# One program order on all engines, from the trunk to the first up tiles, with second steps put off by a product

## The chip, the cores and the metric

The kernel runs on one core of one Trainium2 chip. The metric is device time in microseconds (us) of one execution; a number given for a kernel is the median of several executions. TensorE is called PE, VectorE DVE, ScalarE ACT, GpSimd POOL and SyncE SP, as in the profile.

## The reference

One layer of a streaming encoder is applied to 1024 prompt tokens and to 32 sample tokens, with the same weights, and a last norm follows. All is fp32, the model width is 1024.

```
def trunk_layer(x, attn_core, conv_left, mem_k, mem_v, ...):
    h = rms_norm(x, g_mix)
    q, k, v, ch, cb, cc, ga, gb = jnp.split(h @ w_in, SPLITS, axis=-1)
    a = attn_core(q, k, v) @ w_attn_out              # sliding window, 16 heads of 64
    ...                                              # conv: depthwise, width 3, over cc * ch
    bo = (cb * conv) @ w_conv_out
    x = x + (sigmoid(ga) * a + sigmoid(gb) * bo) @ w_mix_out
    hc = rms_norm(x, g_cross)
    cq = hc @ w_cq                                   # 4 heads of 64
    p = softmax(cq . mem_k * 0.125)                  # 256 memory tokens
    x = x + (p . mem_v) @ w_co
    hm = rms_norm(x, g_mlp)
    x = x + square(relu(hm @ w_up)) @ w_down         # hidden width 4096
```

## The kernel before

Activations lie transposed: 128 features on the partitions, tokens along the free axis. The 1056 tokens are cut into three chunks of 384, 384 and 288 columns; the sample's 32 tokens are the last of chunk 2. Every fp32 operand is split in two fp32r parts, a high part (a copy on ACT) and a low part (source minus high part, on DVE): `split`, lines 115 and 116. A product is one output tile of 128 features for one chunk: eight blocks of the inner dimension with three matmuls each, high weight by high activation, high by low, low by high (`gemm`, lines 167 to 169), 24 matmuls in all. Each weight panel (`wr`) is loaded by SP, split into `wh` and `wl` two products ahead of its use, and for every second panel the low part is kept in DRAM and loaded again for the later chunks (line 141 copies its high part).

The program is a list of items, each a function with the weights it wants; `run` goes through them. A tile scheduler then orders the instructions of each engine, by its own estimates of time. From the trunk to the first up tiles only PE is held to the program's order:

```
in_order = tc.manual_schedule(engines={mybir.EngineType.PE})
```

The **trunk** has eight `conv_out` and eight `mix` products for each chunk. A conv_out product is multiplied by a gate (DVE, line 747), an addend loaded from DRAM is added (POOL, line 748), and the sum is split into M (ACT and DVE, lines 115 and 116). The eight M tiles are the activations of mix. A mix product is added to x (DVE, line 762), scaled by a gain and split into Y (lines 241 and 242), and squared into a running sum (`square_acc`, lines 234 to 238).

Chunk 0's sixteen products come first. After that the products are **fillers**, numbered from 0: chunk 1's sixteen, chunk 2's sixteen, and then the first eight up products of each chunk. `cross_steps(c, base, ...)` hangs the cross-attention of chunk c between them, with base 0, 16 and 32: `at(i, step)` puts a step behind filler i.

- Row statistics: `chunk_col` (at base) sums the squares with a matmul against ones and makes the reciprocal root as a column; `chunk_row` (at base + 1) multiplies an identity by that column, block by block (ACT line 208 for the high part, DVE line 209 for the low part), and two matmuls per block against ones (lines 210 and 211, tile pr) turn it into a row R. The same pair comes again at base + 16 and base + 17 for the MLP's norm, so that the second pair of a chunk and the first of the next stand behind the same fillers.
- `do_cq`: two products for the queries.
- A head, class `Cross`: `scores` (six matmuls of 256 columns, tile sc; line 837), the maximum on DVE (nmx, line 840), three exponentials on ACT (line 842), normalization on DVE; two fillers later `turn` (PE transposes into pt, ACT copies the high part PTh, DVE subtracts the low part PTl); another filler later `values` (tile o, line 873), which is copied, added and split on ACT and DVE (lines 875 to 888). Heads start at the fillers `starts` from base: 3, 5, 7, 9, and 3, 4, 6, 7, 9 in chunk 2, where the sample's head is the first.
- `do_co` (at base + 13 and + 14): two halves of four output tiles each, six matmuls a tile (lines 902 to 904), each followed by an addition to x on DVE (line 906). Two tiles of a half share one PSUM buffer.

`mem_load` (behind filler 0), `mem_load_s` (behind filler 16) and the sample head itself load keys and values through a single buffer `mkr` and split them on ACT and DVE (mkh, mkl, mv). `normed_split` makes the MLP's input of a tile (line 931), stores it, and splits it (lines 933 and 935); eight for chunk 0 lie behind fillers 18 to 25 and eight for chunk 1 behind 34 to 39. `combine_n` and `combine` build sums of such tiles for the paired up products that follow.

## Time and profile before

| | |
|---|---|
| median of 3 runs | 1869.71 us |
| lowest and highest | 1868.11 and 1870.54 us |
| the profiled execution | 1866.0 us |
| its span | 1864.2 us |
| its mean granted PE clock | 0.988 |
| trunk to first up tiles in it | from about 816 to 1232 us |

The profile comes from one execution of its own. Its time is 1.8 us more than the span that the trace covers. A row of a timeline gives the start and the length in us, the engine and the source line, the output and input tiles, their shapes, and in brackets the idle time before it with what ended it. In a row of waits stand the engine, its tile and line, what it waited for, and then the total in us, the number of waits and the longest. A line can be that of a helper: line 116 is every low part that `split` makes, so the tiles' names tell them apart.

### The profile page before, as it was taken

The numbers are of one execution on the slowest core, as the hardware profiler recorded it, in microseconds if no ns is written. First come the engines' busy times: TensorE is split into PE (matmuls) and PEld (weight loads), VectorE is DVE, ScalarE is ACT, GpSimd is POOL, SyncE is SP. The second block draws the span as 40 slices with busy tenths as digits, with TensorE's granted clock in tenths as the row PEclk, the third lists the DMA queues.
The fourth block names the chain that finished last, engine by engine and source line by source line (L and its number), as shares of the span: only waits on it lengthen the run. The fifth ranks groups of instructions, "written<-read, shape, count | busy, mean of one in ns | idle before, by whom it ended". The sixth has DMA issues, their size and how long they took to land. (4 is left out here: it accounts for less than half of the span.)

```text
span 1864.2 us, 29594 instructions
## 1 busy us (share of the span) xinstructions
PE 1808.6 (97%) x11364; PEld 1787.9 (96%) x11364; DVE 1054.8 (57%) x2011; ACT 718.9 (39%) x1414; POOL 351.6 (19%) x381
## 2 busy tenths in 40 slices
PE   7999999999999999999999989899999999999997
PEld 7999999999999999999998889899999999999997
DVE  7766767757654224236575857656555674242255
ACT  8543435334343103223455645532222353030134
POOL 3211010201100000014232221473444000000032
PEclk9999999999999999999999999999999999999998
DMA  4411111212223125146655756643333574131243
GB/s 185 138 64 58 61 55 61 72 51 70 69 81 114 62 92 169 46 142 237 199 184 187 230 183 225 232 162 109 115 97 106 190 248 144 52 116 46 69 146 129
DMA packets 113934, 232.77 MB, mean 125 GB/s; under 512 B 13536, under 2 KB 76672, under 8 KB 113664
## 3 DMA queue, kind: packets, MB, share of 16 engines
q1 hardware_dynamic: 111488, 227.72, 36.5%
q10 hardware_dynamic: 2304, 3.15, 0.5%
q8 instruction: 90, 1.47, 0.3%
q14 instruction: 52, 0.43, 0.1%
HBM read 184.34 MB, written 46.48 MB: 124 GB/s over the span
## 5 line engine op out<-in xcount | busy, mean ns | idle before, releaser
L115 ACT CAST wh<-wr 128x1024 fp32r<-128x1024 f32 x200 | 210.0, 1050 | 503.0 <-PE acc L168 366.7
L167 PE MATMUL acc<-X,wh 128*128 128x384 f32 (+1 forms) x1200 | 390.4, 325 | 6.9 <-ACT wh L115 6.9
L168 PE MATMUL acc<-X,wh 128*128 128x384 f32 (+1 forms) x1200 | 387.8, 323 | 2.2 <-DVE X L242 2.2
L169 PE MATMUL acc<-X,wl 128*128 128x384 f32 (+1 forms) x1200 | 386.8, 322 | 0.3 <-DVE wl L116 0.3
L167 PE MATMUL acc<-Y,wh 128*128 128x384 f32 (+1 forms) x1008 | 328.2, 326 | 0.4 <-ACT Y L933 0.4
L168 PE MATMUL acc<-Y,wh 128*128 128x384 f32 (+1 forms) x1008 | 327.6, 325 | 0.2 <-DVE Y L935 0.2
L169 PE MATMUL acc<-Y,wl 128*128 128x384 f32 (+1 forms) x1008 | 327.1, 325 | 0.0
L116 DVE TENSOR_TENSOR wl<-wr,wh 128x1024 fp32r<-128x1024 f32 x200 | 270.7, 1354 | 65.3 <-ACT wh L115 63.8
L167 PEld LDWEIGHTS acc<-X,wh 128*128 128x128 f32 x1200 | 226.3, 189 | 7.5 <-ACT wh L115 6.9
L168 PEld LDWEIGHTS acc<-X,wh 128*128 128x128 f32 x1200 | 226.5, 189 | 3.9 <-DVE X L242 3.4
L169 PEld LDWEIGHTS acc<-X,wl 128*128 128x128 f32 x1200 | 226.2, 189 | 0.8 <-DVE wl L116 0.8
L167 PEld LDWEIGHTS acc<-Y,wh 128*128 128x128 f32 x1008 | 191.0, 189 | 0.7 <-ACT Y L933 0.7
L168 PEld LDWEIGHTS acc<-Y,wh 128*128 128x128 f32 x1008 | 190.9, 189 | 0.4 <-DVE Y L935 0.4
L169 PEld LDWEIGHTS acc<-Y,wl 128*128 128x128 f32 x1008 | 190.8, 189 | 0.0
L238 POOL TENSOR_TENSOR xacc<-xacc,ct 128x384 f32<-128x384 f32 (+1 forms) x62 | 80.0, 1291 | 366.7 <-ACT ct L236 364.1
L167 PE MATMUL acc<-M,wh 128*128 128x384 f32 (+1 forms) x320 | 106.2, 332 | 2.8 <-ACT M L115 2.8
L168 PE MATMUL acc<-M,wh 128*128 128x384 f32 (+1 forms) x320 | 106.0, 331 | 1.5 <-DVE M L116 1.3
L169 PE MATMUL acc<-M,wl 128*128 128x384 f32 (+1 forms) x320 | 105.5, 330 | 0.0
L748 POOL TENSOR_TENSOR ct<-ct,ld 128x384 f32<-128x384 f32 (+1 forms) x21 | 24.8, 1181 | 382.6 <-DVE ct L747 350.3
L1167 DVE TENSOR_TENSOR Gb<-acc,Gb 128x384 f32<-128x384 f32 (+1 forms) x60 | 31.4, 523 | 112.5 <-PE acc L169 112.5
L115 ACT CAST PTh<-pt 128x512 fp32r<-128x512 f32 (+3 forms) x94 | 46.0, 516 | 123.1 <-PE pt L536 122.2
L167 PE MATMUL acc<-H,wh 128*128 128x288 f32 (+1 forms) x256 | 80.7, 315 | 0.0
(292 smaller groups left out, 3485.7 us busy)
## 6 DMA issues: line engine op xcount, KB each, us to landing
wr<-in_w_down SPq DMA_DIRECT2D x56, 512.0 KB, 3.2
wr<-in_w_in SPq DMA_DIRECT2D x50, 512.0 KB, 3.3
wr<-in_w_up SPq DMA_DIRECT2D x48, 512.0 KB, 3.6
wl<-wl_d SPq DMA_DIRECT2D x28, 512.0 KB, 4.0
wr<-in_w_conv_out SPq DMA_DIRECT2D x24, 512.0 KB, 3.9
wr<-in_w_mix SPq DMA_DIRECT2D x24, 512.0 KB, 4.5
ct<-hid_d SPq DMA_DIRECT2D x64, 192.0 KB, 3.7
hid_d<-lt SPq DMA_DIRECT2D x48, 192.0 KB, 1.9
```

The costliest lines, as they stand in the source:

```text
L115: act.copy(hi, src)
L116: dve.tensor_sub(lo, src, hi.bitcast(F32))
L167: pe.matmul(out, wh[:, a], hi, start=(k == 0), stop=False)
L168: pe.matmul(out, wh[:, a], lo, start=False, stop=False)
L169: pe.matmul(out, wl[:, a], hi, start=False, stop=(k == len(acts) - 1))
L238: pool_e.tensor_tensor(acc, acc, sq, op=ALU.add)
L748: (dve if f == NF - 1 else pool_e).tensor_tensor(t, t, t1, op=ALU.add)
L1167: dve.tensor_add(x, a, x)
```

## The change

Line numbers below are those of the kernel before, unless the diff shows code that is new.

- From the trunk to the first up tiles, PE, DVE, ACT, POOL and SP are all held to the program's order.
- `later(fn)` puts a step on a list; `run` empties it after the next product's weights have been issued and before that product's own steps. Put off in this way are: the split of M (but for the last of eight), the low part of Y and of normed tiles, the low part of the queries, both low parts PTl, the normalization of the scores, the rest of `values` behind its first copy, the splits of the memory keys and values, and the sums of `combine_n` and `combine`.
- Memory keys and values are loaded one by one through two buffers: the prompt's keys behind the fourth, sixth, eighth and tenth product of chunk 0 and its values behind the twelfth and fourteenth, the sample's keys behind the other heads of chunk 2.
- Addends of conv_out and mix are loaded two ahead; one weight panel is fetched ahead of its turn.
- Heads start one filler earlier, the queries' evictions come after both cq products, co comes one filler earlier, and the sample's head is the last of chunk 2.
- The row is made by `row_parts`: the column is split into two parts on DVE, two 384-wide multiplications of a broadcast identity follow, and two matmuls. Its second use per chunk is at base + 16, so that it no longer shares fillers with the next chunk's first.
- ACT's function tables for Exp and Sqrt are loaded by a dummy operation ahead of their use.
- The store of a normed tile goes from ACT's queue to SP's; the low part of N1 goes from POOL to DVE.

```diff
     def run():
         for fn, keys in plan:
-            fn(*[next_w(k) for k in keys])
+            ws = [next_w(k) for k in keys]
+            if keys:
+                put_off_done()
+            fn(*ws)
...
+    def row_parts(c):
+        n, blocks = CH[c][1], BLOCKS[c]
+        pr = ps.tile([P, n], F32, tag="pt", bufs=2, name=nm("pr"))
+        rh, rl = (misc.tile([P, 3], F32R, tag=x, bufs=2, name=nm(x)) for x in ("st_h", "st_l"))
+        dve.tensor_copy(rh, RC[c])
+        dve.tensor_sub(rl, RC[c], rh.bitcast(F32))
+        dh, dl = tmp(n, F32R), tmp(n, F32R)
...
+        for d, r in ((dh, rh), (dl, rl)):
...
+            dve.tensor_tensor(d[:, : full * P].rearrange("p (b t) -> p b t", b=full), eyes, rs, op=ALU.mult)
...
+        pe.matmul(pr, ones_r, dh, start=True, stop=False)
+        pe.matmul(pr, ones_r, dl, start=False, stop=True)
+        return pr
...
+    def split_later(hi, lo, src):
+        act.copy(hi, src)
+        later(lambda: dve.tensor_sub(lo, src, hi.bitcast(F32)))
...
             t = tmp(n)
             dve.tensor_mul(t, a, sg[c][f])
-            (dve if f == NF - 1 else pool_e).tensor_tensor(t, t, t1, op=ALU.add)
             mg[c][f] = (mslot(n), mslot(n))
-            split(*mg[c][f], t)
+            if f == NF - 1:
+                dve.tensor_add(t, t, t1)
+                split(*mg[c][f], t)
+            else:
+                pool_e.tensor_tensor(t, t, t1, op=ALU.add)
+                later(lambda: split(*mg[c][f], t))
...
             for b in range(G):
                 act.activation(stl[:, b], sc[:, b], AF.Exp, bias=nmx[:, b : b + 1], accum_out=den[:, b : b + 1])
-            dve.reciprocal(rec, den)
-            for b in range(G):
-                dve.tensor_scalar_mul(stl[:, b], stl[:, b], rec[:, b : b + 1])
+            def norm():
+                dve.reciprocal(rec, den)
+                for b in range(G):
+                    dve.tensor_scalar_mul(stl[:, b], stl[:, b], rec[:, b : b + 1])
+            later(norm)
...
-                split(ph, pl, pt[:, :, P - w :])
+                split_later(ph, pl, pt[:, :, P - w :])
...
     def normed_split(c, f):
         t = tmp(CH[c][1])
-        pin(dve.scalar_tensor_tensor(t, x1[c][f], col(G_MLP + f), R[c], op0=ALU.mult, op1=ALU.mult))
-        hi, lo = xm[c][f] = (yslot(c), yslot(c))
-        act.copy(hi, t)
-        act.dma_start(xn_d[c][:, f], t)
-        pin(dve.tensor_sub(lo, t, hi.bitcast(F32)))
+        dve.scalar_tensor_tensor(t, x1[c][f], col(G_MLP + f), R[c], op0=ALU.mult, op1=ALU.mult)
+        sp.dma_start(xn_d[c][:, f], t)
+        xm[c][f] = (yslot(c), yslot(c))
+        split_later(*xm[c][f], t)
...
-        two_parts("N1", k, b11, pool_e)
...
+            two_parts("N1", k, b11, dve)
...
-        units = [Cross(c, h) for h in ([0, 1, 2, 3] if c < 2 else [4, 0, 1, 2, 3])]
+        units = [Cross(c, h) for h in ([0, 1, 2, 3] if c < 2 else [0, 1, 2, 3, 4])]
         at(base, lambda: chunk_col(c))
-        at(base + 1, lambda: chunk_row(c))
+        at(base + 1, lambda: chunk_scale(c), lambda: later(lambda: table(AF.Exp)))
         for j in range(2):
-            at(base + 2, (do_cq(c, j), ("w_cq", j)))
+            at(base + 1, (do_cq(c, j), ("w_cq", j)))
...
-        at(base + stats_at, lambda: chunk_col(c))
-        at(base + stats_at + 1, lambda: chunk_row(c))
+        at(base + 14, lambda: later(lambda: table(AF.Sqrt)))
+        at(base + 15, lambda: chunk_col(c))
+        at(base + 16, lambda: chunk_scale(c), all_waiting)
...
-    in_order = tc.manual_schedule(engines={mybir.EngineType.PE})
...
+    in_order = tc.manual_schedule(engines={ET.PE, ET.DVE, ET.Activation, ET.Pool, ET.SP})
...
+        if f in (3, 5, 7, 9):
+            item(lambda h=(f - 3) // 2: load_key(pkeys, mk_d[h // 2, 64 * (h % 2) : 64 * (h % 2) + 64]))
+        if f in (11, 13):
+            item(lambda j=(f - 11) // 2: load_val(pvals, mv_d[j], f"pv{j}"))
-    cross_steps(0, 0, [3, 5, 7, 9], 13, 16)
+    cross_steps(0, 0, [2, 4, 6, 8], 12)
...
-    cross_steps(1, 16, [3, 5, 7, 9], 13, 16)
-    cross_steps(2, 32, [3, 4, 6, 7, 9], 13, 16)
+    cross_steps(1, 16, [2, 4, 6, 8], 12)
+    starts = [2, 3, 5, 6, 8]
+    cross_steps(2, 32, starts, 12)
+    for h in range(4):
+        at(32 + starts[h], lambda h=h: load_key(skeys, io["cmem_k"][h]))
...
     for i, f in enumerate((0, 4, 1, 5, 2, 6, 3, 7)):
-        at(18 + i, lambda f=f: normed_split(0, f))
-        at((34, 35, 35, 36, 37, 37, 38, 39)[i], lambda f=f: normed_split(1, f))
+        at(17 + i, lambda f=f: normed_split(0, f))
+        at(32 + i, lambda f=f: normed_split(1, f))
```

## The prediction

> **What bounds the kernel now.** I began with the page of the profile: how long, and which engine.

> ```profile
> span 1864.2 us, 29594 instructions
> PE 1808.6 (97%) x11364; PEld 1787.9 (96%) x11364; DVE 1054.8 (57%) x2011; ACT 718.9 (39%) x1414; POOL 351.6 (19%) x381
> ```

> TensorE (PE) is busy for 1808.6 of 1864.2 us, so the kernel can only gain what PE idles or runs at a lowered clock. Next I cut the span into stages: ahead of the trunk, the four stretches of the trunk (conv_out and mix of chunk 0 and then the cross-attention of chunks 0, 1 and 2 with the first up tiles), and what follows. The last four rows are short stretches that I use below.

> ```profile
> 0.00:816.00 816.00, 803.12 (x5170) 793.86 (x5171) 465.09 (x1080) 330.14 (x749) 82.62 (x154) 1.00 0.25 86
> 816.00:942.00 126.00, 120.04 (x676) 118.09 (x675) 76.42 (x111) 55.48 (x92) 38.40 (x28) 0.97 0.63 211
> 942.00:1036.00 94.00, 87.27 (x543) 84.86 (x542) 61.88 (x116) 52.88 (x103) 30.44 (x28) 0.98 0.60 195
> 1036.00:1130.00 94.00, 82.27 (x504) 78.83 (x503) 64.55 (x117) 50.75 (x101) 26.23 (x27) 0.93 0.56 188
> 1130.00:1232.00 102.00, 95.44 (x610) 92.84 (x609) 72.29 (x129) 51.19 (x102) 46.17 (x40) 0.97 0.74 251
> 1232.00:1864.00 632.00, 620.46 (x3871) 619.44 (x3869) 314.58 (x461) 178.47 (x269) 127.80 (x106) 0.99 0.36 118
> 929.54:939.98 10.44, 10.44 (x65) 10.41 (x64) 7.76 (x14) 6.26 (x14) 2.03 (x2) 1.00 0.64 213
> 1027.42:1036.42 9.00, 8.81 (x66) 8.36 (x65) 8.88 (x18) 6.73 (x17) 2.37 (x3) 1.00 0.88 281
> 855.40:862.20 6.80, 5.30 (x16) 4.42 (x16) 3.51 (x7) 2.19 (x4) 0.00 (x0) 0.63 0.87 308
> 1114.00:1124.00 10.00, 5.41 (x18) 4.84 (x19) 4.50 (x7) 4.52 (x11) 1.00 (x1) 0.66 0.52 172
> ```

> In each row stand the length, then the busy time of PE, of its weight loads, of DVE, ACT and POOL, and the granted clock. In the trunk PE idles for 6.0 + 6.7 + 11.7 + 6.6 = 31.0 us. One minus the clock, times the length, gives 3.8 + 1.9 + 6.6 + 3.1 = 15.4 us lost to the clock. That is all that a change of the trunk can win, about 46 us. DVE is at 61 to 71% there and ACT at 44 to 56%: neither is full, so in this stage latencies decide, and the order in which a queue meets them. The waits of PE in the trunk say which:

> ```profile
> PE pr L210 <- ACT ct L208: 7.1, 5, 1.9
> PE sc L837 <- ACT mkh L115: 3.5, 1, 3.5
> PE co L902 <- DVE Gb L906: 3.3, 3, 2.1
> PE o L873 <- DVE PTl L116: 3.1, 3, 1.5
> PE acc L167 <- ACT M L115: 2.8, 3, 1.3
> PE co L902 <- DVE Ga L906: 2.8, 3, 1.6
> PE co L902 <- ACT Y L882: 2.1, 1, 2.1
> PE co L903 <- DVE Y L888: 1.8, 3, 0.8
> PE acc L168 <- DVE M L116: 1.3, 2, 1.0
> PE pr L211 <- DVE ct L209: 1.3, 1, 1.3
> PE sc L837 <- DVE mkl L116: 1.1, 1, 1.1
> ```

> Row statistics (pr) cost 7.1 + 1.3 = 8.4 us, the co products 3.3 + 2.8 + 2.1 + 1.8 = 10.0, the sample head's keys (mkh, mkl) 3.5 + 1.1 = 4.6, M between conv_out and mix 2.8 + 1.3 = 4.1, and the low part of the turned scores (PTl, wanted by `values`) 3.1.

> **What the change removes.** Program order on DVE, ACT, POOL and SP changes nothing outside the trunk: the matmuls are the same, and only the three final row statistics differ there, by a chain of about the same length (three ACT and three DVE steps of 128 columns against four DVE steps), which I cost at nothing, within 1 us either way. Inside, the small loads of the keys and values no longer come in one burst through one buffer. How such a load hurts is seen on ACT at the sample head:

> ```profile
> 1118.90 0.40 ACT L115 CAST mkh<-mkr 128x256 fp32r<-128x256 f32 x1 [4.00 <-DMA mkr<-in_cmem_k]
> 1119.32 1.28 ACT L842 ACT_TABLE_LOAD   x1
> ```

> ACT stood for 4.00 us on a key load, and the Exp table came behind it. With the keys one product ahead and the sample head last, 4.6 us of waits go; the table load leaves the chain of the exponentials too, which is already in these gaps. The memory values, which block M in front of the first mix, are loaded during mix instead: I count the whole 4.1 us of the M waits as gone, though a third of it lies at chunk 2's mix and may stay. The 3.1 us on PTl I remove here and count anew below. Together -11.8 us. Two drops of the clock go with them: the stretch at 855.4 lost 0.37 x 6.8 = 2.5 us, the one at 1114 0.34 x 10 = 3.4 us.

> **What program order costs at `values`.** The point to watch is a head that meets a conv_out product. This is chunk 0 before, where nothing stalls: the stretch that begins at 929.54, with the end of a product, has PE busy for 10.44 of 10.44 us. First DVE, then ACT, then PE:

> ```profile
> 929.74 0.56 DVE L747 TENSOR_TENSOR ct<-acc,Gb 128x384 f32<-128x384 f32 x1 [1.24 <-PE acc L169]
> 930.69 1.85 DVE L116 TENSOR_TENSOR wl<-wr,wh 128x1024 fp32r<-128x1024 f32 x1 [0.39 <-ACT wh L115]
> 932.46 0.94 DVE L840 TENSOR_REDUCE nmx<-sc 128x3 f32<-128x768 f32 x1
> 933.33 1.00 DVE L116 TENSOR_TENSOR PTl<-pt,PTh 128x384 fp32r<-128x384 f32 x2
> 934.25 0.54 DVE L116 TENSOR_TENSOR M<-ct,M 128x384 fp32r<-128x384 f32 x1
> ```

> ```profile
> 931.49 0.52 ACT L115 CAST M<-ct 128x384 fp32r<-128x384 f32 x1
> 933.43 0.48 ACT L842 ACTIVATE S<-sc,nmx 128x256 f32<-128x256 f32 x1 [1.43 <-DVE nmx L840]
> ...
> 934.71 0.21 ACT L842 ACTIVATION_READ_ACCUMULATOR S<-sc,nmx 128x1 f32 x1
> 935.16 1.06 ACT L141 CAST wh<-wr 128x1024 fp32r<-128x1024 f32 x1 [0.24 <-ACT S L842]
> ```

> ```profile
> 930.78 0.28 PE L837 MATMUL sc<-mkl,Y 128*128 128x256 f32 x1
> ...
> 935.09 0.34 PE L873 MATMUL o<-PTh,mv 128*128 128x384 f32 x1
> ```

> The scheduler ran M's high part on ACT at 931.49, ahead of the exponentials, and PTl on DVE directly behind nmx; PTl was done at 934.33, 0.8 us before `values` began on PE at 935.09. In the changed program (its order of instructions on each engine) ACT has: PTh twice, three exponentials, the next weight's wh, then M's high part. DVE has: the product's eviction, nmx, M's low part, PTl twice, the normalization. M's low part and PTl are both put off, but M's is first in the list, so PTl stands behind M's low part, that waits for M's high part, and that is behind exponentials and wh. From the rows: scores end at 931.06; nmx 0.94 makes 932.0; exponentials take 934.92 - 933.40 = 1.5, to 933.5; wh 1.06, to 934.6; M high 0.52, to 935.1; M low 0.54, to 935.7; the first PTl, half of 1.00 and a little, to 936.2. `values` wants it 0.17 us after 935.09. That is a wait of 0.9 us without any handing over between engines, and with four or five handovers of about 0.1 us, and the second PTl, 1.4 (bounds 0.9 and 1.8). Chunk 0 has two heads under conv_out, and two under mix, where no M stands in the way but the low part of Y does; I take 0.5 for these. Together 3.8 us. (nmx comes earlier than in the rows because wl now stands elsewhere; that gain is in this walk.)

> In chunk 1 the same happens with products of 288 columns, and DVE also carries the normed splits of chunk 0. The stretch from 1027.42 to 1036.42 is one period there, two products and one head: DVE was busy for 8.88 of 9.00 us, with PE hardly waiting. The same DVE work in program order has a hole in it: from nmx to M's low part DVE waits for 1.5 (exponentials) + 0.5 (Y high, by the row of M high) + 1.06 (wh) + 0.5 (M high) = 3.6 us, of which a multiplication of some 0.6 us (by the eviction's 0.56) fills a part. So the period is about 8.9 + 3.0, and up to 0.7 more for the scores that nmx waits for: 11.9 to 12.6 against 9.0. I take +3.4 for each of three periods and 1.4 for the fourth head, 11.6 us. In the least case the shorter chain is hidden and it is 0; with no overlap between DVE operations it is about 20.

> In chunk 2 five heads meet up products and the normed splits of chunk 1, without M. No row shows this order; between the 0.5 of a head under mix and a full hole of 2.5 I take 1.6 each, the middle: 8 us.

> **The co products.** The second matmul group of a co half waits for the addition of its first group, which stands on DVE behind what the last product left. These two rows give the lengths:

> ```profile
> L116 DVE TENSOR_TENSOR wl<-wr,wh 128x1024 fp32r<-128x1024 f32 x57 | 81.6, 1431 | 13.0 <-ACT wh L115 11.8 <-DMA wl_d<-wl 0.4 <-DMA wr<-in_w_conv_out 0.4
> ```

> ```profile
> L242 DVE SCALAR_TENSOR_TENSOR Y<-Ga,prm,Y 128x384 fp32r<-128x384 f32 x6 | 5.6, 930 | 0.0
> ```

> In program order, counted from the end of the product ahead of the half: eviction 0.8 (from 929.54 to 929.74 plus 0.56), Y high 0.5 (by M high), wh 1.06, wl 1.43, Y low 0.93, the addition 0.56, 5.3 us in all, some 0.3 less where operations of DVE overlap. PE is through its first group of six matmuls after 1.1 (a product's 24 take 4.2, from the scores' end to `values`): 3.9 us. In the other half no Y high and no wh stand in the chain, and wl or Y low alone is ahead: 1.6 us. Three chunks make 16.5 us against 10.0, +6.5. The bound below is -4, because the last head's output is now ready a product earlier and its share of the 10.0 us (2.1 + 1.8) goes; the bound above is +10, if the second half meets wl and Y low both.

> **Row statistics.** The new chain is shorter: eviction 0.8 us after the product's end, two tiny copies of some 0.15 each (no row; taken at a quarter of the 0.56 of a 384-column step), a multiplication of 0.55 to the first matmul and another for the second: PE idles about 1.75 us. But there are now six points instead of four, since the statistics of two chunks no longer share a filler. 6 x 1.75 = 10.5 against 8.4: +2.1. If the broadcast operand makes a multiplication as long as M and eviction together, it is +8; if the copies hide, -1.

> **Moved to other queues.** SP now issues in program order, and the store of the normed tile sits on SP in front of weight loads; SP stands until DVE has written that tile. The cover is the fetch one product ahead; a delay over one product (about 4.2 us from 930.90 to 935.09) would show as ACT waiting for wr. POOL's low part of N1 goes to DVE, in a stage where DVE has room: nothing, or 0.5 us for each of four. The queries' eviction after both cq products: nothing, the scores come a product later.

> **The sum.** -11.8 + 3.8 + 11.6 + 8.0 + 6.5 + 2.1 = +20.2 us of idle PE. The clock: before, 31 us of idle went with 15.4 us lost. Idle would be 51; by proportion 25 us are lost, +10. But most new gaps are short ones, of 1.4 to 1.8 us, and the two drops priced above (5.9 us) go. I take +4, between 0 and +10. The stretch at 855.4 shows that gaps need not be long: PE idled there 1.5 us in all, in pieces, at clock 0.63.

> [...]

> 1866.0 of the profiled execution, 1.8 us more than its span, plus 24.2 is 1890.2, so 1890. The profiled run lies 3.7 us under the median of 1869.71; the prediction is made against the former, and that difference is in the range.

> **Rivals.** (1) Faster: the holes close. It is decided at `values`: if DVE is through M's low part by 934.7 on the clock of the rows above, 1.0 us sooner than walked (a wh of 1.06 that runs ahead of the exponentials and not behind them would give that), PTl is in time and no period lengthens. Then only the removals count: -11.8 idle and -5.9 clock, with co and rows even: 1848. For it speaks that DVE has 29 to 39% free in the trunk; against it the full DVE of the stretch at 1027.42. (2) The cascade: DVE never catches up in chunk 1, the hole is paid without overlap (20 instead of 11.6 us), co at its upper bound (+3.5), rows at theirs (+6), and the clock goes by proportion (+6 more): 1890 + 24 = 1914, to 1925 with chunk 2 in full. (3) The gains and the holes meet: chunk 1 at half its price and chunk 2 at a third, no clock term: 1890 - 6 - 5 - 4 = 1875 down to 1866. (4) The row statistics are not shorter on the path because DVE comes late to them; that moves 2 to 6 us inside the range.

> [...]

> **Chances.** Forecast (1875 to 1905) 0.52; cascade 0.18; a small loss from 1873 to 1875 0.07; within 0.2% 0.04; faster 0.19. A measurement of this kernel tells about 0.2%, 3.7 us. The range reaches from the faster rival's 1848 to 1925, the cascade's end, and leaves out some 0.07 on each side. Slower 0.52 + 0.18 + 0.07 = 0.77.

> **What would show it.** Right: in the waits of PE, `o` waiting for DVE PTl with 15 to 30 us in all instead of 3.1; the gaps on mkh and M gone; six gaps at pr of 1.5 to 2.5 us; DVE idle ahead of M's low part, released by ACT M; a stretch of two products in chunk 1 of 12 us. Wrong: no PTl wait above 0.5 us, and the trunk ending earlier than at 1232; or gaps in which ACT waits for weight loads, which I have at nothing.

## The result and the profile after

| | before | changed |
|---|---|---|
| median | 1868.91 us (4 runs) | 1959.87 us (4 runs, 1957.62 to 1960.65) |
| ratio | | 1.0485, 95% interval 1.0466 to 1.0503 |
| span of the profiled execution | 1864.2 us | 1958.8 us |
| PE busy in it | 1808.6 us | 1837.2 us |
| PE idle in it | 55.6 us | 121.6 us |

The change makes the kernel 91 us slower. The direction was forecast, the size was not: 24 us were. The page of the profile after begins so:

```profile
span 1958.8 us, 29552 instructions
PE 1837.2 (94%) x11364; PEld 1811.5 (92%) x11364; DVE 1038.4 (53%) x2030; ACT 711.6 (36%) x1394; POOL 326.1 (17%) x377
```

The matmuls are as many as before (x11364; a row of the statistics took two matmuls in all before the change too, not two per block). So 28.6 us more of busy PE are the same matmuls at a lower clock (0.970 of full in the mean of the span, 0.988 before), and 66.0 us more are idle. The windows put both in the trunk; the columns are those of the windows of before, so length, PE, weight loads, DVE, ACT, POOL, granted clock:

```profile
0.00:816.00 816.00, 801.80 (x5142) 793.12 (x5143) 464.37 (x1079) 329.46 (x748) 82.86 (x154) 0.99 0.25 83
816.00:900.00 84.00, 74.90 (x421) 71.16 (x419) 37.71 (x51) 26.05 (x37) 19.05 (x18) 1.00 0.54 184
900.00:1000.00 100.00, 87.85 (x473) 85.20 (x474) 55.27 (x102) 48.05 (x92) 22.57 (x22) 0.92 0.49 174
1000.00:1100.00 100.00, 80.76 (x491) 77.45 (x489) 54.45 (x113) 44.59 (x90) 17.40 (x19) 0.90 0.49 168
1100.00:1200.00 100.00, 77.62 (x431) 74.88 (x431) 54.58 (x109) 42.90 (x83) 21.77 (x25) 0.88 0.44 156
1200.00:1340.00 140.00, 106.83 (x613) 103.46 (x612) 60.90 (x118) 48.95 (x91) 44.16 (x44) 0.87 0.54 181
1340.00:1958.00 618.00, 607.43 (x3803) 606.19 (x3801) 311.10 (x461) 171.55 (x254) 118.31 (x96) 0.99 0.36 120
```

Behind 816 us the five trunk windows have PE idle for 9, 12, 19, 22 and 33 us, at clocks down to 0.87. One minus the clock, times the length, is 0 + 8 + 10 + 12 + 18 = 48 us in them, against 15.4 before. The place of 1232 us before now lies near 1327, an estimate that takes what follows as equally long (632 us). DVE is busy for 44 to 55% of these windows, less than the 61 to 71% before: it stands more, it does not work more. PE's main waits in the trunk:

```profile
PE o L946 <- DVE PTl L784: 25.6, 10, 5.6
PE acc L188 <- DMA wl<-wl_d: 13.3, 3, 8.6
PE pr L257 <- DVE ct L254: 13.0, 4, 5.7
PE pr L257 <- DVE ct L256: 7.2, 2, 5.0
PE co L978 <- DVE Gb L982: 6.5, 3, 3.9
PE co L978 <- DVE Ga L982: 5.4, 3, 3.7
PE sc L906 <- DVE Y L882: 5.2, 3, 2.7
PE acc L186 <- ACT wh L115: 5.2, 3, 1.8
PE acc L187 <- DVE Y L784: 4.5, 1, 4.5
PE o L946 <- ACT PTh L783: 4.2, 3, 2.9
PE acc L188 <- DVE wl L116: 2.2, 4, 0.6
PE acc L186 <- ACT wh L142: 1.2, 1, 1.2
```

`values` waits for PTl and PTh for 25.6 + 4.2 = 29.8 us (3.1 before), the rows for 13.0 + 7.2 = 20.2 (8.4), co for 11.9 (10.0), the scores for the queries' low part (Y, line 882) for 5.2, and weights (wh, 5.2 + 1.2, and wl, 13.3 from DRAM and 2.2 from DVE) for 21.9, where the trunk before shows no such wait. A normed tile's low part (Y, line 784) is new with 4.5. The waits on the sample's keys are gone, and those on M are down from 4.1 to 1.8.

The hole at the queue heads is there as drawn. One head in chunk 1, DVE first, then ACT:

```profile
1061.28 0.95 DVE L909 TENSOR_REDUCE nmx<-sc 128x3 f32<-128x768 f32 x1
1062.14 0.61 DVE L1007 SCALAR_TENSOR_TENSOR ct<-Gb,prm,R 128x384 f32<-128x384 f32 x1
1065.44 0.46 DVE L116 TENSOR_TENSOR M<-ct,M 128x288 fp32r<-128x288 f32 x1 [2.69 <-ACT M L115]
1065.82 1.01 DVE L784 TENSOR_TENSOR PTl<-pt,PTh 128x384 fp32r<-128x384 f32 x2
```

```profile
1062.26 0.47 ACT L911 ACTIVATE S<-sc,nmx 128x256 f32<-128x256 f32 x1 [2.27 <-DVE nmx L909]
...
1063.62 0.51 ACT L783 CAST Y<-ct 128x384 fp32r<-128x384 f32 x1
1064.03 1.06 ACT L142 CAST wh<-wr 128x1024 fp32r<-128x1024 f32 x1
1064.97 0.44 ACT L115 CAST M<-ct 128x288 fp32r<-128x288 f32 x1
```

nmx ends at 1062.23; ACT goes through the exponentials, Y's high part, wh and only then M's high part, and DVE stands in front of M's low part for 2.69 us. PTl, whose input had been ready since the turn, follows behind it, and PE waited for it for 5.63 us.

A head without M in the way shows a second form. This is DVE under a mix product of chunk 0:

```profile
977.34 1.23 DVE L116 TENSOR_TENSOR wl<-wr,wh 128x1024 fp32r<-128x1024 f32 x1 [2.51 <-ACT wh L115]
...
979.34 1.01 DVE L784 TENSOR_TENSOR PTl<-pt,PTh 128x384 fp32r<-128x384 f32 x2
```

Here DVE stands for wh, makes the weight panel's low part, then two other low parts, and only then PTl; PE waited for 3.48 us.

SP is the other thing to see. It waits in program order for work of other engines:

```profile
SPq L1013 <- POOL ct L1027: 110.9, 22, 10.0
SPq L147 <- DVE wl L116: 63.9, 7, 13.4
SPq L141 <- PE acc L188: 50.9, 7, 11.3
SPq L1008 <- DVE ct L1007: 45.6, 10, 6.1
```

Line 1013 stores hidden tiles, 1008 normed tiles, 147 the low parts that are kept, and 141 loads such a part, into a buffer that PE must have left. The loads of weight panels stand in the same queue behind these. ACT waited for panels from DRAM for 23.7 us in up products, 15.9 in mix and 14.6 in conv_out, which is what the prediction named as a sign of its being wrong. At the end of the trunk PE itself waits for a kept low part; PE, and SP just ahead of it:

```profile
1304.58 0.61 PE L188 MATMUL acc<-Y,wl 128*128 128x288 f32 x1 [8.62 <-DMA wl<-wl_d]
```

```profile
1294.85 0.32 SPq L1013 DMA_DIRECT2D hid_d<-ct  x1
1295.61 1.75 SPq L1076 DMA_DIRECT2D lt<-xn_d  x4
1297.40 0.42 SPq L1100 DMA_DIRECT2D wr<-in_w_up  x1
1297.92 0.38 SPq L141 DMA_DIRECT2D wl<-wl_d  x1
```

PE had stood since 1295.96, 8.62 us before 1304.58. The last load of wl ahead of that went out at 1297.92, behind a store, four loads of normed tiles and a panel, and took 6.6 us to land (3.8 in the median of the trunk). So the late issue is a part of this wait, and the slow landing another.

### The profile page after: what moved, and what is told of

It reads as the page before. It is cut to its first block, busy times and chain, and to the rows that moved or that the text cites. A ratio compares the mean times of both kernels' runs of the same rounds, so it can differ in the third digit from the quotient of the medians.

```text
span 1958.8 us, 29552 instructions
## 1 busy us (share of the span) xinstructions
PE 1837.2 (94%) x11364; PEld 1811.5 (92%) x11364; DVE 1038.4 (53%) x2030; ACT 711.6 (36%) x1394; POOL 326.1 (17%) x377
## 5 line engine op out<-in xcount | busy, mean ns | idle before, releaser
L115 ACT CAST wh<-wr 128x1024 fp32r<-128x1024 f32 x200 | 209.7, 1050 | 504.6 <-PE acc L187 344.9
L116 DVE TENSOR_TENSOR wl<-wr,wh 128x1024 fp32r<-128x1024 f32 x200 | 263.3, 1317 | 183.5 <-ACT wh L115 183.0
L188 PE MATMUL acc<-Y,wl 128*128 128x384 f32 (+1 forms) x1008 | 335.3, 333 | 14.2 <-DMA wl<-wl_d 13.3
L187 PE MATMUL acc<-Y,wh 128*128 128x384 f32 (+1 forms) x1008 | 334.7, 332 | 4.5 <-DVE Y L784 4.5
L186 PE MATMUL acc<-Y,wh 128*128 128x384 f32 (+1 forms) x1008 | 335.5, 333 | 3.0 <-ACT wh L115 1.8
L188 PEld LDWEIGHTS acc<-Y,wl 128*128 128x128 f32 x1008 | 198.0, 196 | 15.5 <-DMA wl<-wl_d 14.0
L187 PEld LDWEIGHTS acc<-Y,wh 128*128 128x128 f32 x1008 | 197.8, 196 | 5.1 <-DVE Y L784 5.1
L186 PEld LDWEIGHTS acc<-Y,wh 128*128 128x128 f32 x1008 | 198.7, 197 | 3.5 <-ACT wh L115 2.1
L285 POOL TENSOR_TENSOR xacc<-xacc,ct 128x384 f32<-128x384 f32 (+1 forms) x62 | 68.5, 1105 | 365.3 <-ACT ct L283 355.8
L186 PE MATMUL acc<-H,wh 128*128 128x288 f32 (+1 forms) x256 | 80.7, 315 | 0.0
L187 PE MATMUL acc<-H,wh 128*128 128x288 f32 (+1 forms) x256 | 80.5, 314 | 0.0
```

The source lines that it names most:

```text
L115: act.copy(hi, src)
L116: dve.tensor_sub(lo, src, hi.bitcast(F32))
L186: pe.matmul(out, wh[:, a], hi, start=(k == 0), stop=False)
L187: pe.matmul(out, wh[:, a], lo, start=False, stop=False)
L188: pe.matmul(out, wl[:, a], hi, start=False, stop=(k == len(acts) - 1))
L285: pool_e.tensor_tensor(acc, acc, sq, op=ALU.add)
```

## The experiments

Each run was made together with the kernel before on the same chip; the ratios are to that. The edits shown are against the changed kernel, unless the text names the kernel before. Two theories stood against each other at first: H, the hole at the heads of DVE's and ACT's queues, as predicted; S, late weight panels behind SP.

**Which queue.** The runs of the table leave engines to the scheduler by one line; the two of the kernel before add engines to its line instead, and drop the pins that kept the steps of normed tiles in order:

```diff
-    in_order = tc.manual_schedule(engines={ET.PE, ET.DVE, ET.Activation, ET.Pool, ET.SP})
+    in_order = tc.manual_schedule(engines={...})
```

| engines in program order | median us | ratio, 95% interval |
|---|---|---|
| changed kernel, all five | 1959.87 | 1.0485, 1.0466 to 1.0503 |
| all but SP | 1918.80 | 1.0281, 1.0251 to 1.0311 |
| PE, DVE, ACT | 1919.34 | 1.0267, 1.0245 to 1.0289 |
| PE, SP | 1892.52 | 1.0140, 1.0110 to 1.0169 |
| PE, DVE | 1881.03 | 1.0064, 1.0038 to 1.0091 |
| PE | 1867.27 | 0.9998, 0.9982 to 1.0015 |
| PE, ACT | 1851.43 | 0.9898, 0.9869 to 0.9927 |
| kernel before, all five | 2065.50 | 1.1067, 1.1032 to 1.1102 |
| kernel before, PE, ACT | 1899.44 | 1.0161, 1.0139 to 1.0183 |

All but SP:

> The changed kernel with SP left to the scheduler (PE, DVE, ACT and POOL stay in program order). Theory H (the hole at the head of DVE's and ACT's queues, as predicted): the holes stay, only the waits on weight loads go that PE shows directly (7 us in chunk 0, 15 us in the up products): 1935 to 1945 us. Theory S (SP in program order brings the weight panels late, and wh and then wl block ACT and DVE behind them): most of the excess goes, 1885 to 1900 us; DVE's waits of wl on wh fall from 130 us to under 40.

Measured 1918.8 us, between the two; DVE's waits of wl on wh are 84.8 us, also between. SP's order is worth 41 us of the 91; the larger part stays without it. PE's first waits in that run are those of H:

```profile
PE o L946 <- DVE PTl L784: 26.3, 11, 5.6
PE pr L257 <- DVE ct L254: 9.9, 4, 3.2
```

29.8 us at `values` (with 3.5 on PTh), as with all five in order, but the rows are down from 20.2 to 9.9 + 2.6 and the weights from 21.9 to 5.5. In chunk 1 nearly the same gaps stand at the same products in both runs (5.63 us twice, 2.87 and 2.88; one at PTh is 2.94 against 1.35): SP adds elsewhere, at the start, at two rows and at the up products.

PE alone, and PE with SP:

> The changed kernel with only PE in program order, as before; steps put off, staged loads, shorter row statistics and moved heads stay. Theory H and theory S agree that the excess goes: 1850 to 1870 us. If the moved steps themselves cost (six row points, co), it stays above 1875.

> The changed kernel with PE and SP in program order, DVE, ACT and POOL left to the scheduler. Theory H: near the run with PE alone, within 10 us. Theory S: more than half of the 91 us is there, 1915 us or more, unless DVE and ACT, ordered by the scheduler, work around a late panel: then 1875 to 1900.

With PE alone the changed kernel is as fast as before, 1867.27 us against 1868.10: without the order of the other engines, all the moved steps together neither win nor lose. The waits on keys are gone there, and the rows take 15.7 us instead of 8.4, so the gain on the keys is given back. SP's order alone costs 25 us, in the range for a DVE and an ACT that work around a late panel. 25 and 51 (all but SP, over PE alone) are less than the 93 of all five: behind queues in order a late panel costs more.

The kernel before in the same order:

> The kernel before with nothing but the order of all five engines taken from the program (the pins that order normed splits fall away, since program order holds them). No step is put off here, so second steps stand directly behind their first. Both theories: slower than the changed kernel, 1980 to 2060 us, by what putting off is worth; if it is under 1960, putting steps off lost time.

2065.5 us, 5 us beyond the slow end of the range. The rest of the change, with the steps put off, the staged loads, the shorter row and the moved heads, is worth 106 us inside this order; it does not make the order cheap. What each of these parts is worth was not measured.

DVE alone and ACT alone:

> The changed kernel with PE and DVE in program order only. Theory H: the hole needs M's high part behind the exponentials on ACT; with ACT free it is filled, so 1875 to 1895. If DVE's order alone makes the loss (51 us without SP), 1905 or more.

> The changed kernel with PE and ACT in program order only. Theory H: DVE free can run PTl ahead of M's low part, so most of the loss goes: 1867 to 1885. If ACT's order alone makes the loss, 1905 or more.

1881 and 1851 us. DVE's order costs 14 us over PE's alone, within H's range. ACT's order costs nothing: it gains 16 us, more than expected, and it beats both kernels. The loss comes when both queues are in order: 14 - 16 turns into +52. POOL was still open:

> The changed kernel with PE, DVE and ACT in program order; POOL and SP left to the scheduler. Alone, DVE's order costs 14 us over PE's (1881 against 1867) and ACT's gains 16 (1851). If the loss is the meeting of both queues, this is within 6 us of the run without SP (1919 us); if POOL's order had a part in it, 1865 to 1905.

1919.34 us against 1918.80: with SP free, POOL's order has no part in it.

The kernel before with ACT in order:

> The kernel before with PE and ACT in program order, nothing put off, keys and values loaded as before. If ACT's order by itself brings the 16 us, 1850 to 1860. If it needs the steps put off and the staged loads, ACT stands at the keys and at M's addition on POOL: 1880 or more.

1899.44 us, so the gain from ACT's order needs the rest of the change. Which part of it is not shown: PE's longest wait there is 20.2 us at pr on ACT's line 208, in a kernel where ACT still makes the rows, and its waits on keys are 9.7 + 0.7.

**What fills the hole.** PTl directly behind its high part, with SP left to the scheduler:

```diff
-                split_later(ph, pl, pt[:, :, P - w :])
+                split(ph, pl, pt[:, :, P - w :])
```

> The changed kernel with SP left to the scheduler (as in the run without SP, 1919 us) and PTl not put off: it stands on DVE directly behind its high part, ahead of nmx and of M's low part. Theory H: the waits of `values` on PTl and PTh fall from 30 us to under 8 and the time to 1880 to 1895. Rival (DVE is simply full, a hole closed here opens elsewhere): the waits turn up at the scores, the turns or the co products, and the time stays above 1905.

1904.84 us (ratio 1.0184, 1.0151 to 1.0217), 14 us better than all but SP, and short of H's 1880 to 1895. PE's waits on PTl fell to 2.4 us, but those on PTh rose to 9.3, and 4.6 on tO and 4.1 on M opened: the rival was half right. PTl behind M was not the whole of the hole. In the run without SP, DVE waited for wh, at the head of wl, for 84.8 us, against 19 with PE alone. So the next two, with PE, DVE and ACT in order, put the weights behind the put-off steps:

```diff
-            ws = [next_w(k) for k in keys]
             if keys:
                 put_off_done()
+            ws = [next_w(k) for k in keys]
```

> PE, DVE and ACT in program order (1919 us), and the put-off steps run ahead of the next weights' issue instead of behind it: on ACT M's high part stands directly behind the exponentials, with wh behind it; on DVE wl stands behind PTl and the normalization. Theory H1 (what holds the queues is wh behind the exponentials, and wl behind wh): DVE's 83 us of waits of wl on wh fall under 50, PE's 30 us at `values` under 18, the time 1885 to 1900. Theory H2 (the exponentials alone hold them, wh only passes the time on): above 1908.

> The same, with PTl at once behind its high part as well. Alone that was worth 14 us (1919 to 1905). If the two causes add, 1870 to 1886; if they are the same hole closed twice, no better than the better of the two alone.

Weights last gives 1883.27 us (ratio 1.0084, 1.0055 to 1.0113), from 1919.34, a little better than H1's range. These rows are PE's first two waits in that run, and then DVE's wait for wh with PE, DVE and ACT in order and in that run:

```profile
PE pr L257 <- DVE ct L254: 11.4, 4, 3.5
PE o L946 <- DVE PTl L784: 10.9, 6, 4.4
```

```profile
DVE wl L116 <- ACT wh L115: 83.0, 52, 4.2
DVE wl L116 <- ACT wh L115: 45.9, 44, 3.4
```

From 83 to 45.9 us for wh and from 29.7 to 12.2 at `values` (with 1.3 on PTh), both as H1 said. The gap of 3.48 us at the mix product shown above is gone; that of 5.63, where PTl stands behind M, is 4.42. With PTl at once too it is 1886.98 us, no better: the same hole closed twice. So the place of the weight split, ahead of the put-off steps of a head, is 36 of the 52 us that DVE's and ACT's order costs. Of the 35 us between the two profiled executions 19.6 are idle PE (17.5 at `values`) and 15.7 busy PE, at a mean clock of 0.985 against 0.975. What the same edit does with PE alone in order was not run, so a part of the 36 us could be a gain that needs no order. The 16 us that are left over PE alone I have not taken apart.

**What SP's order does.** All five engines in order, and two panels fetched ahead instead of one, up to filler 44 and one from there on:

```diff
-        if ahead[0] and not fetched and wpos[0] < len(worder) and worder[wpos[0]] is not STOP:
+        while len(fetched) < int(ahead[0]) and wpos[0] + len(fetched) < len(worder) and worder[...] is not STOP:
             fetch_w()
```

> The changed kernel, all five engines in order, with two weight panels fetched ahead of their turn instead of one, up to filler 44. Theory S1 (the panel's fetch comes too late behind a blocked SP): ACT's waits on panel loads fall from 54 us to under 25 and the time from 1960 to 1920 to 1940. Theory S2 (what comes late are the kept low parts, loaded from DRAM behind stores, and the loss is at the up products): the 13 us on wl stay, 1950 or more.

1938.83 us (1.0365, 1.0335 to 1.0396), in S1's range; ACT's waits on panels fell from 54 to 20 us, all that is left at the up panels, and the 13.3 us on kept low parts stayed (13.9), as S2 said of them. Then, on top of it, the stores, put off by a product as well:

```diff
-        sp.dma_start(xn_d[c][:, f], t)
+        later(lambda: sp.dma_start(xn_d[c][:, f], t))
...
-            hidden(c, j, h)
+            if ahead[0]:
+                later(lambda: hidden(c, j, h))
+            else:
+                hidden(c, j, h)
```

> All five engines in order, two panels fetched ahead (1939 us), and the stores of normed and hidden tiles put off by one product, so that SP reaches them when DVE or POOL has written. If what is left of SP's share is SP standing at these stores, the 14 us of PE on kept low parts (wl) and ACT's 19 us on up panels go and the time comes to that without SP, 1917 to 1925. If SP stands at the loads of kept low parts, that wait for PE, it stays above 1932.

1917.47 us (1.0257, 1.0222 to 1.0292), with SP in order as good as without it. The wait on wl fell to 5.0 us and ACT's on up panels to 9.2. So SP's 41 us are two things of about equal size: 21 us for a fetch of one panel that stood behind other waits, and 21 us for stores at the head of SP's queue. The two were measured in this order alone, the second on top of the first.

**A faster version.** With PE and ACT in order the rows were left as PE's largest wait, 6.1 + 2.8 + 2.0 us. Making the scaled identities one product earlier:

```diff
-        at(base, lambda: chunk_col(c))
+        at(base, lambda: chunk_col(c), lambda: row_cols(c))
...
-        at(base + 15, lambda: chunk_col(c))
+        at(base + 15, lambda: chunk_col(c), lambda: row_cols(c))
...
-        at(39 + k, lambda k=k: combine_n(k))
-        at(48 + k, lambda k=k: combine(k))
+        at(40 + k, lambda k=k: combine_n(k))
+        at(49 + k, lambda k=k: combine(k))
```

Here `row_cols` is the DVE half of `row_parts`; the two matmuls stay where they were.

> The changed kernel with PE and ACT in order (1851 us), the scaled identities of the rows made one product earlier, directly behind their column, and combine and combine_n one filler later. The waits at pr fall from 10.9 us to under 3 and the last co half's 5.2 us go: 1834 to 1842. If DVE, ordered by the scheduler, puts the identities behind the evictions anyway, 1848 to 1853.

1837.72 us (4 runs), ratio 0.9820, 0.9794 to 0.9845, faster than both kernels. The rows' waits:

```profile
PE co L978 <- DVE Gb L982: 6.5, 3, 5.2
PE pr L257 <- DVE ct L254: 6.1, 4, 2.6
PE pr L257 <- DVE ct L256: 2.8, 2, 1.9
PE pr L258 <- DVE ct L254: 2.0, 3, 0.8
```

```profile
PE co L986 <- DVE Ga L990: 4.8, 3, 3.5
PE co L986 <- DVE Gb L990: 3.7, 3, 2.4
PE pr L265 <- DVE ct L253: 2.3, 2, 1.7
PE pr L265 <- DVE ct L255: 2.1, 1, 2.1
```

The first fence is the kernel with PE and ACT in order, the second the faster version. pr falls from 10.9 to 4.4 us, not under 3. co falls from 9.2 (with 1.9 and 0.8 in two smaller rows) to 8.5, and its longest gap from 5.2 to 3.5; the move of combine and that of the rows were made in one run, so what each did is not shown apart. The idle of PE falls from 48.6 to 40.8 us and its busy time from 1801.9 to 1795.7, at a mean clock of 0.992 against 0.990.

## Why the prediction was wrong

Its range ended at 1925 us and the time is 1959.87. Against the profiled execution 24.2 us were forecast and 94.6 us came. By its own steps:

- **What the change removes: right.** 4.6 us on keys went in full and of M's 4.1 us 2.3 went (1.6 + 0.2 are left); with SP free all of it. The run with PE alone shows that these gains are not kept by themselves, since the rows take back more than the keys give.
- **`values`: right in mechanism, somewhat low.** 3.8 + 11.6 + 8.0 = 23.4 us were forecast and 29.8 measured, the same with SP in order and without. By chunk it is 3.8, 11.6 and 8.0 forecast and 5.6, 16.3 and 7.9 measured. The hole of 3.0 us measured 2.69 at the head shown, and the two products around it took 11.8 us (DVE evicts at 1056.42 and at 1068.21), where 11.9 to 12.6 were drawn. The handover between engines, the author's estimate of 0.1 us without a row, is 0.03 there (nmx ends at 1062.23, the exponential starts at 1062.26). What the walk missed is that wl stands at DVE's head too, behind wh: it walked M and PTl and treated wl as gone elsewhere ("wl now stands elsewhere"). So a head under mix was priced at 0.5, and the one shown cost 3.48. The runs with the weights behind the put-off steps show the place of the weight split as the larger part of what DVE and ACT cost together.
- **co: too high.** 16.5 forecast, 11.9 measured.
- **Row statistics: mis-sized.** 6 x 1.75 = 10.5 forecast; 12.5 without SP, 20.2 with it, in six gaps of 2.0 to 5.7 us instead of 1.5 to 2.5. In the chain the copy (0.16 us in the median) and the multiplication (0.55) were sized well; the column's low part, taken at 0.15, took 0.78 in the median (0.16 to 0.98). For the rest, what came late was its start.
- **"Moved to other queues": the step that failed.** SP's program order was costed at nothing, on the cover of a fetch one product ahead. It is 41 us, and without SP in order the time, 1918.8, lies inside the range. That cover is used up by SP standing for a store (up to 10.0 us at a time) or at a kept low part whose buffer PE has not left (up to 18.0), where I had checked the normed store alone; stores of hidden tiles and loads of kept low parts I did not cost. The queries' eviction, also at nothing, is 5.2 us on the scores (3.2 without SP); a normed tile's low part, which no term has, is another 4.5.
- **The clock: mis-sized.** +4 us were taken of 0 to +10, because new gaps would be short; that short gaps lower the clock less was the author's estimate, which no row of before shows. Busy PE rose by 28.6 us with 66.0 us of idle, 0.43 for each; without SP by 18.4 with 35.4, 0.52. By the prediction's own measure, one minus the clock times the length, 33 us more are lost in the trunk with 65 us more of idle, the same half as the 15.4 to 31.0 of before. The proportion would have been nearer than the discount for short gaps.

Added up from PE's waits without SP, the terms leave 35 us of idle where 20.2 were forecast: `values` 6 too low, weights at 5.5, the scores at 3.2 and a normed tile at 2.9 with nothing put down for them, rows 2 too low, co 5 too high. That the time without SP falls into the range is therefore partly the range's width.

The rivals: the cascade was the nearest, and it too left out SP. The faster one was decided as it said, at `values`, and fell there. That ACT's order by itself is a gain was no rival at all.

## What to carry to other kernels

When several engines are put into program order, cost each queue alone and then each pair: here ACT's order gained 16 us, DVE's lost 14, and both together lost 52, where a step that waits at the head of one queue is what the other queue is waiting for. A DMA queue in order needs the same walk as an engine (SP's order cost 41 us here): list what every transfer on it waits for, and ask how long the loads behind it stand. Holding ACT alone beside PE in order, and preparing a short chain a product before its use, was faster than either kernel here (1837.72 us); holding DVE alone was not (1881.03).

## What the runs showed of the hardware

```profile
896.43:899.85 3.42, 1.04 (x5) 0.40 (x3) 1.24 (x2) 1.45 (x2) 0.00 (x0) 1.00 1.00 321
899.85:903.26 3.41, 3.37 (x11) 3.37 (x12) 2.53 (x5) 2.04 (x3) 2.08 (x2) 0.50 1.04 416
910.08:913.50 3.42, 1.19 (x6) 0.67 (x5) 2.83 (x6) 0.00 (x0) 0.99 (x1) 1.00 0.83 262
913.50:916.91 3.41, 3.41 (x12) 3.41 (x11) 0.53 (x1) 2.07 (x4) 0.00 (x0) 0.50 0.69 261
```

In the first, PE idles for 2.38 of 3.42 us, in gaps of 1.78 and 0.60; the 3.41 us behind it run at half the clock. In the third it idles for 2.23, nearly all in one gap at pr, and again half the clock follows. The 46 us ahead of the first hold 6.7 us of idle PE, more thinly spread, at the full clock. In this trunk all 18 stretches at half the clock begin right behind 3.41 us with at least 1.88 us of idle PE, and full-clock windows on the same steps of 3.41 us with 1.55 or less were not followed by one. In the trace of before the border is less sharp: 1.41 us at 1065.4 was followed by half the clock, 1.86 at 898.2 was not. The stretch at 855.4 in the prediction has to be read the same way: the clock was half from 857.20 to 864.03, behind 2.34 us of idle in the 3.41 us before.

The halved clock followed on gaps of 1.78 and 0.60 us together, and on one of 2.21. The changed kernel has nine trunk gaps of more than 3.41 us, 44.0 us together; in the faster version PE's longest wait in the trunk is one of 3.5 us, and its PE was busy 12.9 us less than before (1795.7 against 1808.6). What exactly lowers the clock is not settled by these runs.
